# Order of the matrix products inside a weight unit, and one value projection of width 512 in place of two of width 256

## Chip, core, metric

The kernel runs on one core of one Trainium2 chip. The metric is the device time of one execution in microseconds (us), the median of several runs.

## What is computed

A decoder trunk of two layers over 256 positions and 2048 channels, all in float32. Layer 0 (even) has sliding-window attention (A, 16 heads) beside dilated attention (B, 8 heads in three pattern groups that are merged by their softmax denominators); layer 1 (odd) has stick-breaking attention (C) and latent attention (D). Each layer ends with a squared-ReLU MLP of width 8192. Cut to what matters here:

```python
# even layer, w_in is 2048 x 5888; the three dilated groups gi = 0, 1, 2
h = x @ w_in                                       # 256 x 5888
qa, ka, va, hb = split(h, [1024, 1152, 1280])
for gi, (window, dil) in enumerate(((128, 1), (512, 4), (2048, 16))):
    q, k, v = hb[:, gi*1536:(gi+1)*1536] as 3 x 8 heads x 64
    o[gi], lse[gi] = banded_attention(q, k, v, dilation=dil)
ob = sum over gi of softmax(lse)[gi] * o[gi]
x = layer_norm(ALPHA * x + concat(oa, ob) @ w_out)
# every layer
hid = relu(x @ w1);  x = layer_norm(ALPHA * x + (hid * hid) @ w2)
```

## The kernel before

**Weights.** All weights stream through one list, made by `plan` in the order of use. An entry, here called a unit, is 128 x 1024 float32: `block(w, k0, nkt, c0, width)` cuts a column band of the matrix into units of 1024/width row tiles of 128 (a unit of width 512 has two row tiles, of width 256 four). SyncE loads a unit into `raw`; ScalarE casts it to `w_hi` (L120) and VectorE stores the remainder in `w_lo` (L121). Four pairs of `w_hi`, `w_lo` are kept (`spl`), and units are split three ahead of their use.

**Products.** An operand is held as a high and a low part, and a product is hi*hi + hi*lo + lo*hi, summed in PSUM. Two helpers do nearly all of TensorE's work:
- `ws` has the weights as the stationary operand (128 x 128, loaded by one LDWEIGHTS for each product). An activation tile is 128 x 512: 256 columns of high part, then 256 of low part. For each output tile f and each row tile kk it issues one 512-column product of `w_hi` with both parts (L326) and then one 256-column product of `w_lo` with the high part into the upper half of the same bank (L327). A call has a bank for each f. At the last unit, each bank is handed to `take` as soon as it is complete; `take` uses ScalarE and VectorE to join its halves. `ws` serves the query and key projections and the first matrix of both MLPs.
- `as_` has the activations as the stationary operand and streams the weights: three products for each row tile and each half t of the positions (L372 to L374), of the width of the unit. It serves values, output projections and the second matrix of the MLPs.

**Attention steps.** Between two units of a projection the code calls `pump()`, which runs one step of the attention queue on all engines (`attn_step`): the scores of a pair of heads (L694), one transpose of a finished probability tile through the single PSUM tile `pt` (L260, `flip`) with ScalarE's copy to `pT` (L262), or the product of two probability tiles with the values (L279, L281, `weigh`). Steps have a fixed lag behind one another, and one transpose goes out in a step. The queue thus runs in the shadow of the projections, so long as there are units left; `finish(job)` runs the remaining steps one after the other without units between them. An engine takes its instructions in the order in which the code issues them.

**The dilated heads.** `even_b(half, ...)` runs twice, for four heads each. For each group gi it projects q and k (two `ws` calls of width 256), queues the scores, and projects v (`as_`, width 256, four units, each followed by a pump). After the second half come the output projections: columns c = 0, 1 over ten of twelve tiles, then c = 2 over all twelve. The last two tiles are those of the second half; `finish(jb[1])` runs when c = 2 first asks for one, which is ahead of the products of its fifth unit (through `near`, L372's loop).

Of the kernel before, what the change touches and what calls it, by code (L numbers as in the profile page):

```python
# [11 lines left out]
F32 = mybir.dt.float32  # L12
# [6 lines left out]
P = 128  # L19
S = 256  # L20
D = 2048
KT = D // P
# [12 lines left out]
def alibi(n):  # L35
    return [float(v) for v in np.float32(2.0) ** (np.float32(-8.0) * np.arange(1, n + 1, dtype=np.float32) / np.float32(n))]
# [127 lines left out]
class Trunk:  # L164
# [140 lines left out]
    def ws(self, xs, nkt, width, take, more=False):  # L305


        nc = self.nc
        nf = width // P
        if more:  # L310
            banks = [self.ps.tile([P, 512], F32, name=n, bufs=m) for n, m in (("sc", 2), ("sc", 2), ("pt", 1), ("o", 1))]
        else:
            banks = [self.acc() for _ in range(nf)]
        kt = 0
        while kt < nkt:
            self.near(xs, kt, 1024 // width, nkt)
            end = kt + 1024 // width >= nkt
            hi, lo, n, wd = self.w.next(ahead=self.split_ahead - end)
            assert wd == width
            self.near(xs, kt + 2, 1024 // width, nkt)  # L320
            for f in range(nf):
                for kk in range(n):
                    xh, xl, both = xs[kt + kk]
                    c = kk * width + f * P
                    first, last = kt + kk == 0, kt + kk == nkt - 1
                    nc.tensor.matmul(banks[f], hi[:, c:c + P], both, start=first, stop=False, skip_group_check=True)  # L326
                    nc.tensor.matmul(banks[f][:, S:2 * S], lo[:, c:c + P], xh, start=False, stop=last, skip_group_check=True)  # L327
                if kt + n == nkt:
                    take(f, banks[f])
            kt += n  # L330
            if kt < nkt:
                self.pump()
# [47 lines left out]
    def plan(self):  # L380
        a, w = self.a, self.w
        wi = a["even_w_in"][0]
        w.block(wi, 0, KT, 0, 512)
        w.block(wi, 0, KT, 512, 512)
        w.block(wi, 0, KT, 1024, 256)
        for half in range(2):
            for gi in range(3):
                for j in range(3):
                    w.block(wi, 0, KT, 1280 + gi * 1536 + j * 512 + half * 256, 256)
        wo = a["even_w_out"][0]  # L390
        for c in range(3):
            w.block(wo, 0, 10 if c < 2 else 12, c * 512, 512)
        for c in range(2):
            w.block(wo, 10, 2, c * 512, 512)
        w.block(wo, 0, 12, 3 * 512, 512)
        self.plan_mlp(0)
        wi = a["odd_w_in"][0]
        w.block(wi, 0, KT, 3072, 512)
        w.block(wi, 0, KT, 3584, 288)
        w.block(wi, 0, KT, 2048, 512)  # L400
        w.block(wi, 0, KT, 0, 512)
        self.plan_uq(0, 0)
        w.block(wi, 0, KT, 1024, 512)
        self.plan_uq(0, 1)
        w.block(wi, 0, KT, 2048 + 512, 512)
        self.plan_ukv(0)
        w.block(wi, 0, KT, 512, 512)
        self.plan_uq(1, 0)
        w.block(wi, 0, KT, 1024 + 512, 512)
        self.plan_uq(1, 1)  # L410
        self.plan_ukv(1)
        wo = a["odd_w_out"][0]
        for k0s in ((0, 8), (4,), (12,)):
            for c in range(4):
                for k0 in k0s:
                    w.block(wo, k0, 4, c * 512, 512)
        self.plan_mlp(1)
# [324 lines left out]
    def even(self):  # L742
        nc = self.nc
        slopes = alibi(16)
        qa = self.project(512, scale=0.125) + self.project(512, scale=0.125)
        kd = self.tile2()
        va = self.tile2()
        kvf = self.at.tile([P, 2, S], F32, name="kvf", bufs=1)
        vf = kvf[:, 1, :]

        def take(f, bank):
            self.join(kvf[:, f, :], bank)
            if f == 0:
                for kv in range(2):
                    for half in range(2):
                        eng = nc.scalar.copy if half else nc.vector.tensor_copy
                        eng(kd[half * HD:half * HD + HD, kv, :], kvf[kv * HD:kv * HD + HD, 0, :])

        self.ws(self.xT, KT, 256, take)
        self.pump()  # L760

        def flip_v():
            pt = self.ps.tile([P, 384], F32, name="pt")
            for t in range(2):
                nc.tensor.transpose(pt[:, t * P:(t + 1) * P], vf[:, t * P:(t + 1) * P], self.ident)
            nc.vector.tensor_copy(va[:, :, 0:P], pt[:, 0:S].rearrange("p (t c) -> p t c", t=2))

        self.at_step(self.i, 0, flip_v)
        top, power, divide = self.softmax(1, sink=lambda h: self.sinks[:, h:h + 1])

        def score(h, u):
            r = slice((h % 2) * HD, (h % 2) * HD + HD)
            return qa[h // 4][r, (h // 2) % 2, :], kd[r, h // 8, :]

        def bias(h, u, sc, st):
            nc.vector.scalar_tensor_tensor(st, self.masks[:, 0, :], -slopes[h], sc, op0=ALU.mult, op1=ALU.add)
            top(h, st)

        def value(h, u, blk):
            return va[:, blk, (h // 8) * HD:(h // 8) * HD + HD]  # L780

        ja = Job("A", 16, 1, score, (bias, power, divide), value, 5, self.y_at)
        self.queue(ja)
        jb = [self.even_b(0, self.y_at), self.even_b(1, self.x_slot)]
        self.finish(jb[0])
        self.finish_side()
        ys = ja.out + jb[0].out
        st = self.new_stats()

        def rest():  # L790
            self.finish(jb[1])
            yield jb[1].out

        late = LazyTiles(rest())
        late.tiles += ys
        for c in range(3):
            o = self.as_(late if c == 2 else ys, 12 if c == 2 else 10, 512)
            self.add_res(o, c, True, st if c == 2 else None)
            self.pump()
        for c in range(2):  # L800
            o = self.as_(jb[1].out, 2, 512)
            self.add_res(o, c, False, st)
        o = self.as_(late, 12, 512, hold=2)
        return (o, 3, True), st

    def even_b(self, half, y):
        nc = self.nc
        sl = alibi(8)
        qkv = []
        top, power, divide = self.softmax(3)  # L810

        def score(h, u):
            r = slice((h % 2) * HD, (h % 2) * HD + HD)
            return qkv[u][0][r, h // 2, :], qkv[u][1][r, h // 2, :]

        def bias(h, u, sc, st):
            nc.vector.scalar_tensor_tensor(st[:, u * 384:(u + 1) * 384], self.masks[:, 1 + u, :], -sl[half * 4 + h], sc,
                                           op0=ALU.mult, op1=ALU.add)
            if u == 2:
                top(h, st)  # L820

        def value(h, u, blk):
            return qkv[u][2][:, blk, h * HD:h * HD + HD]

        job = Job(f"B{half}", 4, 3, score, (bias, power, divide), value, 4, y)
        for gi in range(3):
            q = self.project(256, scale=0.125)[0]
            k = self.project(256)[0]
            qkv.append((q, k, None))
            self.queue(job, gi)  # L830
            o = self.as_(self.xT, KT, 256)
            v = self.tile2()
            for t in range(2):
                nc.scalar.copy(v[:, t, :], o[t])
            self.pump()
            qkv[gi] = (q, k, v)
        return job

    def project(self, width, tag="qk", scale=1.0):
# [334 lines left out]
```

## Time and profile before

| | |
|---|---|
| median of 3 runs | 2205.27 us (2204.86 to 2205.53) |
| the profiled execution: its time | 2207.19 us |
| its span (first to last instruction) | 2205.4 us |
| outside the span | 1.79 us |
| TensorE busy | 2181.4 us (99%), 11611 products |
| weight loads busy (beside the products) | 1833.6 us (83%) |
| VectorE, ScalarE busy | 1400.8 us (64%), 1058.4 us (48%) |
| bytes moved | 399.07 MB, 181 GB/s mean |

A product's duration in the profile holds its way through the array, and products overlap: what a product costs TensorE is the distance from its start to the start of the next, which the timeline shows. The granted TensorE clock was 0.998 of the full 2.4 GHz over the span.

### The profile page before, as it was taken

What the parts mean: (1) busy time and instruction counts of PE and PEld (TensorE: products, weight loads), DVE (VectorE), ACT (ScalarE), POOL (GpSimd) and SP (SyncE); (2) the same over time, 40 slices, a digit from 0 to 9 for tenths busy, and PEclk for the clock granted to TensorE, in tenths of its full rate; (3) what the DMA queues carried; (4) which work ended last, traced back from release to release, by engine and by line L of the source; (5) the groups of instructions that cost most, each with busy time, mean ns of one, the idle gap of its engine ahead of it and who ended that gap; (6) DMA issues with size and microseconds to landing.
All of it is one profiled execution on the core that took longest, in us unless ns stands there. A gap on an engine that the chain in (4) does not pass through costs nothing.

```text
span 2205.4 us, 30048 instructions
## 1 busy us (share of the span) xinstructions
PE 2181.4 (99%) x11611; PEld 1833.6 (83%) x11612; DVE 1400.8 (64%) x1904; ACT 1058.4 (48%) x1524; POOL 53.7 (2%) x80
## 2 busy tenths in 40 slices
PE   9999999999999999999999999999999999999998
PEld 7888887888888888888888787778888888888886
DVE  5766465775465556565567887878645655554656
ACT  4555453444354345344344565635534534443542
POOL 0000000000000000000012101000000000000000
PEclk9999999999999999999999999999999999999999
DMA  7445554565555555555557443455555555556553
GB/s 266 152 137 158 155 171 155 194 198 191 191 183 197 192 185 190 194 179 198 192 154 227 151 130 135 144 197 190 213 195 182 188 196 189 191 192 191 179 198 121
DMA packets 224320, 399.07 MB, mean 181 GB/s; under 512 B 12778, under 2 KB 56512, under 8 KB 223408
## 3 DMA queue, kind: packets, MB, share of 16 engines
q1 hardware_dynamic: 221472, 386.78, 52.9%
q0 software_dynamic: 2416, 9.84, 1.6%
q8 instruction: 91, 1.49, 0.3%
q10 hardware_dynamic: 288, 0.52, 0.1%
q14 instruction: 53, 0.43, 0.1%
HBM read 395.00 MB, written 2.10 MB: 180 GB/s over the span
## 4 chain that ended last, share of the span: by engine, by line
PE 92%; DVE 4%; issue 1%; DMA 1%; ACT 1%; POOL 0%; SPq 0%; POOLq 0%; ACTq 0%; DVEq 0%
PE acc L326 19%; PE acc L372 14%; PE acc L373 14%; PE acc L374 14%; PE acc L327 9%; PE sc L326 5%; PE sc L327 3%; PE pt L326 3%; PE o L326 3%; DVE w_lo L121 1%; PE pt L327 1%; PE o L327 1%; PE sc L694 1%; PE pt L260 1%; PE o L279 1%
## 5 line engine op out<-in xcount | busy, mean ns | idle before, releaser
L121 DVE TENSOR_TENSOR w_lo<-raw,w_hi 128x1024 fp32r<-128x1024 f32 (+2 forms) x748 | 890.9, 1204 | 606.5 <-ACT w_hi L120 602.3
L120 ACT CAST w_hi<-raw 128x1024 fp32r<-128x1024 f32 (+2 forms) x748 | 760.3, 1030 | 759.7 <-PE acc L374 451.5
L326 PE MATMUL acc<-x,w_hi 128*128 128x512 f32 x1824 | 655.5, 402 | 3.4 <-DVE x L515 3.1
L327 PE MATMUL acc<-x,w_lo 128*128 128x256 f32 x1824 | 513.0, 281 | 0.0
L326 PEld LDWEIGHTS acc<-x,w_hi 128*128 128x128 f32 x1824 | 343.9, 189 | 91.4 <-issue 3.6
L372 PE MATMUL acc<-w_hi,h_hi 128*128 128x512 f32 x1016 | 395.4, 389 | 0.0
L373 PE MATMUL acc<-w_lo,h_hi 128*128 128x512 f32 x1016 | 395.3, 389 | 0.0
L374 PE MATMUL acc<-w_hi,h_lo 128*128 128x512 f32 x1016 | 395.3, 389 | 0.0
L327 PEld LDWEIGHTS acc<-x,w_lo 128*128 128x128 f32 x1824 | 345.7, 190 | 0.4
L372 PEld LDWEIGHTS acc<-w_hi,h_hi 128*128 128x128 f32 x1016 | 190.7, 188 | 39.9
L374 PEld LDWEIGHTS acc<-w_hi,h_lo 128*128 128x128 f32 x1016 | 190.7, 188 | 39.7
L373 PEld LDWEIGHTS acc<-w_lo,h_hi 128*128 128x128 f32 x1016 | 190.7, 188 | 39.2
L326 PE MATMUL sc<-x,w_hi 128*128 128x512 f32 x512 | 186.7, 399 | 0.0
L327 PE MATMUL sc<-x,w_lo 128*128 128x256 f32 x512 | 143.8, 281 | 0.0
L372 PE MATMUL acc<-w_hi,x 128*128 128x256 f32 (+2 forms) x400 | 135.6, 339 | 0.3 <-DVE x L514 0.2
L373 PE MATMUL acc<-w_lo,x 128*128 128x256 f32 (+2 forms) x400 | 132.5, 331 | 0.2 <-DVE w_lo L121 0.2
L374 PE MATMUL acc<-w_hi,x 128*128 128x256 f32 (+2 forms) x400 | 132.6, 331 | 0.0
L326 PEld LDWEIGHTS sc<-x,w_hi 128*128 128x128 f32 x512 | 96.2, 188 | 24.1
L338 ACT ACTIVATE xfull<-acc 128x256 f32<-128x256 f32 x130 | 49.7, 384 | 127.1 <-PE acc L327 108.6
L327 PEld LDWEIGHTS sc<-x,w_lo 128*128 128x128 f32 x512 | 96.7, 189 | 0.0
L326 PE MATMUL pt<-x,w_hi 128*128 128x512 f32 x256 | 96.3, 399 | 0.0
L326 PE MATMUL o<-x,w_hi 128*128 128x512 f32 x256 | 96.2, 399 | 0.0
(203 smaller groups left out, 2089.0 us busy)
## 6 DMA issues: line engine op xcount, KB each, us to landing
raw<-in_mlp_w SPq DMA_DIRECT2D x512, 512.0 KB, 3.8
raw<-in_even_w_in SPq DMA_DIRECT2D x92, 512.0 KB, 4.2
raw<-in_odd_w_in SPq DMA_DIRECT2D x56, 512.0 KB, 3.6
raw<-in_odd_w_out SPq DMA_DIRECT2D x32, 512.0 KB, 3.5
raw<-in_even_w_out SPq DMA_DIRECT2D x24, 512.0 KB, 3.8
gb_rows<-in_ln_g POOLq DMA_DIRECT2D x3, 1024.0 KB, 5.0
gb_rows<-in_ln_b POOLq DMA_DIRECT2D x3, 1024.0 KB, 7.1
raw<-in_odd_w_uq SPq DMA_DIRECT2D x8, 384.0 KB, 4.3
```

The costliest lines, as they stand in the source:

```text
L120: nc.scalar.copy(h, r)
L121: nc.vector.tensor_tensor(l, r, h.bitcast(F32), op=ALU.subtract)
L260: nc.tensor.transpose(pt[:, b * P:(b + 1) * P], st[:, u * 384 + b * P:u * 384 + (b + 1) * P], self.ident)
L279: nc.tensor.matmul(o[rows, :], v, w[:, 0:S], start=first, stop=False, skip_group_check=True)
L326: nc.tensor.matmul(banks[f], hi[:, c:c + P], both, start=first, stop=False, skip_group_check=True)
L327: nc.tensor.matmul(banks[f][:, S:2 * S], lo[:, c:c + P], xh, start=False, stop=last, skip_group_check=True)
L338: nc.scalar.activation(t, bank[:, S:2 * S], AF.Copy, scale=scale)
L372: nc.tensor.matmul(outs[t], xh[:, ts], hi[:, c:c + width], start=first, stop=False, skip_group_check=True)
L373: nc.tensor.matmul(outs[t], xh[:, ts], lo[:, c:c + width], start=False, stop=False, skip_group_check=True)
L374: nc.tensor.matmul(outs[t], xl[:, ts], hi[:, c:c + width], start=False, stop=last, skip_group_check=True)
L694: nc.tensor.matmul(sc[:, cols], q[:, qs], k[:, ks], start=True, stop=True, skip_group_check=True)
```

## The change

In `ws`, the products of a unit are put in another order. In a unit that is not a call's last, first all eight 512-column products (f outer, kk inner) and then all eight 256-column ones. In the last unit each f has its 512-column products and then its 256-column ones, ahead of its `take`: runs of two (width 512) or four (width 256). No product is added or taken away.

In the dilated heads, the values of both halves are projected in half 0, with units of width 512 (eight of two row tiles in place of two times four of four). The second half's values are kept in three new tiles `vb`. Half 1 has no value projection and so no pumps from one. `as_` itself is as before; its three products are L375 to L377 in the changed file, and those of `ws` L326 and L329.

```diff
     def ws(self, xs, nkt, width, take, more=False):
...
-            for f in range(nf):
-                for kk in range(n):
-                    xh, xl, both = xs[kt + kk]
-                    c = kk * width + f * P
-                    first, last = kt + kk == 0, kt + kk == nkt - 1
-                    nc.tensor.matmul(banks[f], hi[:, c:c + P], both, start=first, stop=False, skip_group_check=True)
-                    nc.tensor.matmul(banks[f][:, S:2 * S], lo[:, c:c + P], xh, start=False, stop=last, skip_group_check=True)
-                if kt + n == nkt:
-                    take(f, banks[f])
+            ends = kt + n == nkt
+            for fs in ([[f] for f in range(nf)] if ends else [range(nf)]):
+                todo = [(f, kk, kk * width + f * P) for f in fs for kk in range(n)]
+                for f, kk, c in todo:
+                    nc.tensor.matmul(banks[f], hi[:, c:c + P], xs[kt + kk][2], start=kt + kk == 0, stop=False,
+                                     skip_group_check=True)
+                for f, kk, c in todo:
+                    nc.tensor.matmul(banks[f][:, S:2 * S], lo[:, c:c + P], xs[kt + kk][0], start=False,
+                                     stop=kt + kk == nkt - 1, skip_group_check=True)
+                if ends:
+                    take(fs[0], banks[fs[0]])
...
     def plan(self):
...
-                for j in range(3):
+                for j in range(2):
                     w.block(wi, 0, KT, 1280 + gi * 1536 + j * 512 + half * 256, 256)
+                if half == 0:
+                    w.block(wi, 0, KT, 1280 + gi * 1536 + 1024, 512)
...
     def even_b(self, half, y):
...
-            o = self.as_(self.xT, KT, 256)
-            v = self.tile2()
-            for t in range(2):
-                nc.scalar.copy(v[:, t, :], o[t])
-            self.pump()
-            qkv[gi] = (q, k, v)
+            if half == 0:
+                o = self.as_(self.xT, KT, 512)
+                vs = [self.tile2(), self.at.tile([P, 2, S], F32, name="vb", bufs=3)]
+                for j, v in enumerate(vs):
+                    for t in range(2):
+                        nc.scalar.copy(v[:, t, :], o[t][:, j * S:(j + 1) * S])
+                self.vb.append(vs[1])
+                self.pump()
+                qkv[gi] = (q, k, vs[0])
+            else:
+                qkv[gi] = (q, k, self.vb[gi])
```

**A unit on TensorE.** These are rows of TensorE's program in the first query projection, its third unit, before. A row names the line, the operation, the bank `acc` that is written, the activation tile `x2` and the split weights; the two row tiles of the unit share a name.

```order
L502 MATMUL sc_214<-ident_88,x_res_90 128x128 x4
L326 MATMUL acc_117<-x2_181,w_hi_168 128x512
L327 MATMUL acc_117<-x2_181,w_lo_169 128x256
L326 MATMUL acc_117<-x2_181,w_hi_168 128x512
L327 MATMUL acc_117<-x2_181,w_lo_169 128x256
L326 MATMUL acc_118<-x2_181,w_hi_168 128x512
L327 MATMUL acc_118<-x2_181,w_lo_169 128x256
```

The same unit in the changed program, whole (`x2` at the end of a row: two in a row that read alike):

```order
L507 MATMUL sc_214<-ident_88,x_res_90 128x128 x4
L326 MATMUL acc_117<-x2_181,w_hi_168 128x512 x2
L326 MATMUL acc_118<-x2_181,w_hi_168 128x512 x2
L326 MATMUL acc_119<-x2_181,w_hi_168 128x512 x2
L326 MATMUL acc_120<-x2_181,w_hi_168 128x512 x2
L329 MATMUL acc_117<-x2_181,w_lo_169 128x256 x2
L329 MATMUL acc_118<-x2_181,w_lo_169 128x256 x2
L329 MATMUL acc_119<-x2_181,w_lo_169 128x256 x2
L329 MATMUL acc_120<-x2_181,w_lo_169 128x256 x2
```

The widths alternated product by product; now they change twice in a unit of sixteen products.

**The end of the dilated heads.** These are the last attention steps of half 1 on TensorE before, ahead of the fifth unit of column c = 2 of the output projection (`y`: attention outputs; S: probability tile):

```order
L260 MATMUL pt<-ident,S 128x128 x3
L372 MATMUL acc<-w_hi,y 128x512
L373 MATMUL acc<-w_lo,y 128x512
L374 MATMUL acc<-w_hi,y 128x512
...
L279 MATMUL o<-pT,qk 64x256 x2
L281 MATMUL o<-pT,qk 64x128 x2
L372 MATMUL acc<-w_hi,y 128x512
```

And the last steps of half 1 in the changed program, in the same place:

```order
L377 MATMUL acc<-w_hi,y 128x512
L279 MATMUL o<-pT,vb 64x256 x2
L281 MATMUL o<-pT,vb 64x128 x2
L260 MATMUL pt<-ident,S 128x128 x6
L279 MATMUL o<-pT,vb 64x256 x2
L281 MATMUL o<-pT,vb 64x128 x2
L260 MATMUL pt<-ident,S 128x128 x3
L279 MATMUL o<-pT,vb 64x256 x2
L281 MATMUL o<-pT,vb 64x128 x2
L375 MATMUL acc<-w_hi,y 128x512
```

Before, twelve products of a unit or more stood between any two transposes of half 1. Now half 1's last value projection and its four pumps are gone, and `finish` still has four steps to run, so that two of the transposes (the row with `x6` is two tiles of three) and two `weigh` steps have no unit before them.

## Rows read from the trace of the kernel before

**Rows 1.** The page: busy time by engine; the chain by engine, by line.
```profile
PE 2181.4 (99%) x11611; PEld 1833.6 (83%) x11612; DVE 1400.8 (64%) x1904; ACT 1058.4 (48%) x1524; POOL 53.7 (2%) x80
...
PE 92%; DVE 4%; issue 1%; DMA 1%; ACT 1%; POOL 0%; SPq 0%; POOLq 0%; ACTq 0%; DVEq 0%
```

**Rows 2.** Groups by line and form: operation, shapes, count; busy us, mean ns; idle before.
```profile
L326 PE MATMUL acc<-x,w_hi 128*128 128x512 f32 x1824 | 655.5, 402 | 3.4 <-DVE x L515 3.1
...
L372 PE MATMUL acc<-w_hi,x 128*128 128x256 f32 x192 | 55.9, 291 | 0.0
...
L326 PEld LDWEIGHTS acc<-x,w_hi 128*128 128x128 f32 x1824 | 343.9, 189 | 91.4 <-issue 3.6 <-ACT w_hi L120 2.9 <-DVE x L515 2.7
```

**Rows 3.** Timeline, TensorE, MLP's first matrix: start us, duration, line, operation.
```profile
440.07 0.40 PE L326 MATMUL sc<-x,w_hi 128*128 128x512 f32 x1
440.31 0.28 PE L327 MATMUL sc<-x,w_lo 128*128 128x256 f32 x1
440.42 0.40 PE L326 MATMUL sc<-x,w_hi 128*128 128x512 f32 x1
...
464.45 0.40 PE L326 MATMUL acc<-x,w_hi 128*128 128x512 f32 x1
```

**Rows 4.** Timeline, TensorE, MLP's second matrix: products of 512 columns alone.
```profile
739.65 0.39 PE L373 MATMUL acc<-w_lo,h_hi 128*128 128x512 f32 x1
...
760.27 0.39 PE L374 MATMUL acc<-w_hi,h_lo 128*128 128x512 f32 x1
```

**Rows 5.** Timeline, TensorE, a value projection: products of 256 columns alone.
```profile
273.91 0.28 PE L373 MATMUL acc<-w_lo,x 128*128 128x256 f32 x1
...
279.43 0.28 PE L374 MATMUL acc<-w_hi,x 128*128 128x256 f32 x1
```

**Rows 6.** Timeline, TensorE, layer 1's `ukv`: twelve 256-column products, then six of 512.
```profile
1277.20 0.28 PE L997 MATMUL acc<-y,w_hi 128*128 128x256 f32 x1
...
1278.14 0.28 PE L996 MATMUL acc<-y,w_hi 128*128 128x256 f32 x1
...
1278.50 0.40 PE L1002 MATMUL acc<-w_hi,y 128*128 128x512 f32 x1
...
1279.66 0.39 PE L1004 MATMUL acc<-w_hi,y 128*128 128x512 f32 x1
```

**Rows 7.** Timeline, TensorE: first 512-column runs after alternation, at two places.
```profile
495.89 0.40 PE L372 MATMUL acc<-w_hi,h_hi 128*128 128x512 f32 x1
...
498.45 0.39 PE L374 MATMUL acc<-w_hi,h_lo 128*128 128x512 f32 x1
...
673.43 0.40 PE L372 MATMUL acc<-w_hi,h_hi 128*128 128x512 f32 x1
...
674.59 0.39 PE L374 MATMUL acc<-w_hi,h_lo 128*128 128x512 f32 x1
```

**Rows 8.** Timeline, TensorE: from a run of 512 columns to a 256-column product.
```profile
582.99 0.39 PE L326 MATMUL acc<-x,w_hi 128*128 128x512 f32 x1
583.22 0.28 PE L327 MATMUL acc<-x,w_lo 128*128 128x256 f32 x1
583.33 0.40 PE L326 MATMUL acc<-x,w_hi 128*128 128x512 f32 x1
```

**Rows 9.** Timeline, TensorE and ScalarE, a late attention step in the output projection.
```profile
361.33 0.55 PE L260 MATMUL pt<-ident,S 128*128 128x128 f32 x3
361.64 0.48 PE L372 MATMUL acc<-w_hi,y 128*128 128x512 f32 x1
361.95 0.40 PE L373 MATMUL acc<-w_lo,y 128*128 128x512 f32 x1
...
364.27 0.39 PE L374 MATMUL acc<-w_hi,y 128*128 128x512 f32 x1
...
361.97 0.48 ACT L262 COPY pT<-pt 128x384 f32<-128x384 f32 x1 [2.63 <-PE pt L260]
362.35 1.05 ACT L120 CAST w_hi<-raw 128x1024 fp32r<-128x1024 f32 x1
```

More of the change, by code (lines that the diff above doesn't have):

```diff
@@ L780, in value @@
             return va[:, blk, (h // 8) * HD:(h // 8) * HD + HD]
+        self.vb = []
         ja = Job("A", 16, 1, score, (bias, power, divide), value, 5, self.y_at)
```

## Prediction

> **What bounds the kernel.** I read the page first. TensorE is busy 99% of the span and carries 92% of the chain that ended last [rows 1]; VectorE, ScalarE and the transfers have a third of their time or more to spare. So the time is the number of products times what each costs TensorE, and only that. The groups by line then say which products there are, but their mean durations (402 ns for 512 columns, 291 for 256 [rows 2]) can't be added: products overlap. The timeline gives the cost, from start to start. In `ws`, where the widths alternate, 69 pairs lie between the first and the last row of [rows 3]: 24.38 us, or 353.3 ns a pair. Where only 512-column products follow each other, 91 steps take 20.62 us, 226.6 ns each [rows 4]. Where only 256-column ones do, 46 steps take 5.52 us, 120.0 ns each [rows 5]. One of each, unmixed, would be 346.6 ns: **alternation costs 6.7 ns a pair**. The operands differ between these rows (in [rows 3] weights are stationary, in [rows 4, 5] activations), but the twelve 256-column products of `ukv` at the start of [rows 6] are stationary weights, and end at the same 0.12 us.
>
> **Part 1, the order in `ws`.** By the code, `ws` is called 38 times with width 512 (8 units) and 13 times with width 256 (4 units); each unit has 8 pairs, 2848 in all, of which the 1824 of [rows 2] write `acc` and the rest the banks `sc`, `pt` and `o`. All have the order changed: 38 x 7 + 13 x 3 = 305 units get runs of eight, 51 last units get runs of two or four.
>
> A run of eight costs 8 x 346.6 = 2773 ns against 8 x 353.3 = 2826 now, so 53 ns could come back, if a change of width were free. The rows say it isn't quite. After 256-column products, 512-column ones start slowly: the five steps from 1278.50 to 1279.66 [rows 6] take 1.16 us, 27 ns more than 5 x 226.6, before they settle. The same 27 ns stand after alternation in the second pair of [rows 7] (1.16 us for five), while the first pair there has 2.56 us for eleven steps, 67 ns too much. The other change costs nothing: from the last 512-column product of a run to the 256-column one is 0.23 us, and the next step only 0.11 [rows 8], 10 ns under 120; the first eight steps of [rows 6] are 0.94 us, 20 ns under. So a unit pays between 0 and 67 ns, less 0 to 20. I take 27, seen right behind a 256-column run, less the 10 of [rows 8]: 2790 ns, **36 ns saved a unit**.
>
> Counted on the changed program, 63 of the 305 units come right after an attention step or a layer norm's transposes. There 512-column products stay slow for longer: ten steps from 361.95 to 364.27 take 2.32 us, 5.4 ns too much each [rows 9], so 43 ns for eight in place of 27; I take 20 ns saved. For a last unit of width 512 there are four changes of width with runs of two; by the first two steps of a slow start (0.24 and 0.23, some 14 ns) less 10 it saves up to 36 ns, by nothing but the pairs that stop alternating (4 of 8) 27, by the slower start of [rows 7] nothing. I take 13. Sum: 242 x 36 + 63 x 20 + 51 x 13 = 8.7 + 1.3 + 0.7 = **10.7 us less**. The bounds: with free changes 305 x 53 + 51 x 27 = 17.5 us less; with 67 ns and no credit each unit loses 14 ns, 4.3 us more.
>
> The first thing a reader should ask is whether a product covers the load of the next weights. A LDWEIGHTS record lasts 189 ns [rows 2], longer than the 120 ns step of the 256-column products, and yet these keep their 120 ns; so the record isn't what a load holds up. The Trainium skill, "TensorE: Matmul & The Clock Gate", section "LDWEIGHTS (loading the stationary operand)", gives a load the number of its columns over 1.2 GHz, an estimate of 107 ns for 128. By that rule every product here covers the next load in either order, the order has no say, and part 1 would be nothing; by the rows it is 10.7 us. The rows don't contradict the 107 ns, but the 6.7 ns of alternation and the slow starts have no place in it.
>
> Nothing else on the path moves with the order. `w_lo` is wanted later in a unit than before and `w_hi` is given back earlier; both were ready in time (TensorE stood idle 3.4 us in all ahead of 1824 of the first products of a pair, for an activation tile [rows 2]). Each `take` keeps its place behind its own bank.
>
> **Part 2, the values.** For each group, 192 products of 256 columns become 96 of 512: 96 x (2 x 120.0 - 226.6) = 1.29 us, 3.9 us for three. Seven of the 24 new units follow transposes and pay 12 x 5.4 = 65 ns each, 0.5 us, so **3.4 us less**. The units of the weight stream are as many and as large; the twelve copies out of PSUM are the same number, on ScalarE, off the path.
>
> **The steps that lose their cover.** Half 1 loses four pumps behind its last scores, so four steps that ran between units are left to `finish`. Their work on TensorE is not new; what is new is that TensorE waits for ScalarE, as there is one `pt` tile. Covered, a transpose starts at 361.33, its copy at 361.97 for 0.48 us, and behind it ScalarE has a cast of 1.05 us [rows 9]. Uncovered, the transpose after it can't start before about 1.2 us where 0.31 would do: 0.85 us idle. The cast issued for the fifth unit stands ahead of the second copy, which ends some 2.65 us after the first transpose; `weigh` fills until 2.3: 0.4 us idle. The last `weigh` waits for the third copy: 0.85 us. Together **2.1 us more**; at least 0.8 (one wait), at most 4 if a cast gets ahead of each copy. Behind it the `y` copy and subtraction have the fifth unit's twelve products (2.7 us) as cover.
>
> **Sum.** -10.7 - 3.4 + 2.1 = -12.0 us. The profiled execution took 2207.19 us (span 2205.4 and 1.79 around it) and would take 2195.2. The median of the three runs is 1.92 us under the profiled one; I carry the difference over: **2193.3 us**.
>
> **Rivals.**
> 1. *Order makes no difference.* The 6.7 ns belong to the products of `ws` (two widths into one bank) or every unit gives back 53 ns at its changes of width, near the 67 of [rows 7]. For it: no row shows eight stationary-weight products of 512 columns in a run. Against it: [rows 6] with 27. Left are -3.4 + 2.1: 2204.0 us. The Trainium skill's rule on loads, above, comes out at the same time.
> 2. *Changes of width are free.* A unit's 256-column run gains what the 512-column run loses, as the 0.94 us in [rows 6] suggest (20 of 27). Then -17.5, -3.9 and only 0.8 for the tail: 2184.7 us.
> 3. *Slower.* Each return from 256 to 512 columns pays the long start, 67 ns in eleven steps. The point from which it decides is 53 ns a unit. At 67 the 305 units lose 4.3 us; the 38 last units of width 512, with four returns each (two first steps of 0.24 us, 25 ns, nothing given back), lose some 46 ns each, 1.7 us; with part 2 and the tail +4.7 us: 2210.0 us. For it: the first pair of [rows 7]. Against: of the eight switches from `ws` to the MLP's second matrix in the timeline only two look like it, the other six like the second pair.
>
> **Chances.** The forecast (a unit saves 20 to 45 ns) 0.62, with its own range 2188 to 2199; rival 1 0.17; rival 2 0.15; rival 3 0.06. 0.2% of the time is 4.4 us, about what a measurement of this kernel can tell from no change, so faster means under 2200.9: the forecast, rival 2 and a little of rival 1's spread, 0.79; same 0.16; slower 0.05. The range reaches to rival 1 and to rival 2: 2185 to 2204.
>
> **What would show it.** In the timeline of a `ws` unit: eight starts 226 to 236 ns apart, settling, then one step of about 0.11 us and seven of 0.117 to 0.120, a unit of 2.79 us where it was 2.83. The MLP's first matrix (2048 of the pairs) should shorten by some 8 us of part 1. In the value projections: 512-column steps of 0.227 in half 0, none in half 1. Ahead of the fifth unit of column c = 2: three waits of TensorE between transposes of under a microsecond each, with the clock still granted in full. The prediction is wrong if a run of eight 512-column products keeps steps of 0.235 to its end, if 256-column runs fall over 0.12, or if the tail waits several microseconds.

## The result and the profile after

The changed kernel takes 2194.11 us (median of 6 runs, 2193.77 to 2194.51) against 2205.58 us (6 runs beside it, 2204.86 to 2206.26): a ratio of 0.9948, 95% interval 0.9935 to 0.9961. It is 11.5 us faster; 12.0 were forecast, and 2193.3 us.

The page after, busy time by engine and the chain by engine [rows 1]:

```profile
PE 2165.6 (99%) x11324; PEld 1818.2 (83%) x11324; DVE 1398.8 (64%) x1904; ACT 1057.8 (48%) x1524; POOL 53.5 (2%) x80
...
PE 92%; DVE 4%; issue 1%; DMA 1%; ACT 1%; POOL 0%; SPq 0%; POOLq 0%; ACTq 0%; DVEq 0%
```

TensorE bounds the kernel as before, and has 287 products fewer on record (288 by the program: 576 of 256 columns became 288 of 512).

A unit of the MLP's first matrix, in the timeline of TensorE (start, duration of the merged row, line, count). Before, such a unit was a row for each product [rows 3]:

```profile
581.14 2.00 PE L326 MATMUL acc<-x,w_hi 128*128 128x512 f32 x8
582.98 1.12 PE L329 MATMUL acc<-x,w_lo 128*128 128x256 f32 x8
583.93 2.00 PE L326 MATMUL acc<-x,w_hi 128*128 128x512 f32 x8
...
588.57 1.11 PE L329 MATMUL acc<-x,w_lo 128*128 128x256 f32 x8
```

Read the starts, not the durations: eight 512-column products take 1.84 us, where eight unmixed ones [rows 4] would take 1.813, and eight 256-column ones 0.95, where unmixed ones [rows 5] would take 0.96. The unit is 2.79 us; it was 2.83. The slow start of 27 ns and the credit of 10 ns were read from other places before [rows 6 to 8], and here they stand.

A call's last unit, in runs of two, takes 2.79 us as well, from its first row to the first of the next unit:

```profile
597.90 0.63 PE L326 MATMUL acc<-x,w_hi 128*128 128x512 f32 x2
598.37 0.39 PE L329 MATMUL acc<-x,w_lo 128*128 128x256 f32 x2
...
600.69 1.09 PE L326 MATMUL sc<-x,w_hi 128*128 128x512 f32 x4
```

The best ruler in these traces is one MLP quarter: 512 products, from the first product of `ws` to the first of the second matrix. Before it was 582.99 to 673.43 [rows 7, 8], 90.44 us. After:

```profile
578.37 1.98 PE L326 MATMUL acc<-x,w_hi 128*128 128x512 f32 x8
...
667.71 0.40 PE L375 MATMUL acc<-w_hi,h_hi 128*128 128x512 f32 x1
```

89.34 us, 1.10 less. The timeline holds six quarters of this kind, each with the same gain, and two that begin with a layer norm's transposes and gain some 1.35 us each: 9.3 us of the whole.

The end of the dilated heads on TensorE, where before a unit followed each transpose [rows 9]:

```profile
359.64 0.65 PE L279 MATMUL o<-pT,vb 128*64 128x256 f32 x4
...
360.44 0.55 PE L260 MATMUL pt<-ident,S 128*128 128x128 f32 x3
361.61 0.55 PE L260 MATMUL pt<-ident,S 128*128 128x128 f32 x3 [0.62 <-ACT pT L262]
362.09 0.65 PE L279 MATMUL o<-pT,vb 128*64 128x256 f32 x4
...
362.94 0.55 PE L260 MATMUL pt<-ident,S 128*128 128x128 f32 x3
363.41 1.12 PE L279 MATMUL o<-pT,vb 128*64 128x256 f32 x3
...
364.90 0.50 PE L375 MATMUL acc<-w_hi,y 128*128 128x512 f32 x1
```

The same stretch on ScalarE:

```profile
361.08 0.48 ACT L262 COPY pT<-pt 128x384 f32<-128x384 f32 x1 [2.63 <-PE pt L260]
361.46 1.05 ACT L120 CAST w_hi<-raw 128x1024 fp32r<-128x1024 f32 x1
362.40 0.48 ACT L262 COPY pT<-pt 128x384 f32<-128x384 f32 x1
363.58 0.48 ACT L262 COPY pT<-pt 128x384 f32<-128x384 f32 x1 [0.69 <-PE pt L260]
```

The second transpose starts 1.17 us after the first, and its row names the copy it waited for. The third comes right behind `weigh`, without a wait. The last `weigh` takes from 363.41 to 364.90, 1.49 us, where a covered one takes 0.80 (359.64 to 360.44): its second head's copy starts only at 363.58. From 360.44 to 364.90 are 4.46 us; three transposes of 0.31 [rows 9] and two `weigh` of 0.80 are 2.53. So the uncovered steps cost up to 1.9 us; some 0.3 of it is given back, since four returns from a step to a unit are gone, each with a first product of 0.31 us in place of 0.23 [rows 9].

### The profile page after: what moved, and what is told of

The parts are those of the page before. It is cut to its first block, busy times and chain, and to the rows that moved or that the text cites. A ratio compares the mean times of both kernels' runs of the same rounds, so it can differ in the third digit from the quotient of the medians.

```text
span 2191.9 us, 29478 instructions
## 1 busy us (share of the span) xinstructions
PE 2165.6 (99%) x11324; PEld 1818.2 (83%) x11324; DVE 1398.8 (64%) x1904; ACT 1057.8 (48%) x1524; POOL 53.5 (2%) x80
## 4 chain that ended last, share of the span: by engine, by line
PE 92%; DVE 4%; issue 1%; DMA 1%; ACT 1%; POOL 0%; SPq 0%; POOLq 0%; ACTq 0%; DVEq 0%
PE acc L326 19%; PE acc L375 14%; PE acc L377 14%; PE acc L376 14%; PE acc L329 10%; PE sc L326 5%; PE sc L329 3%; PE pt L326 3%; PE o L326 3%; PE o L329 1%; PE pt L329 1%; DVE w_lo L121 1%; PE sc L699 1%; PE pt L260 1%; PE o L279 1%
## 5 line engine op out<-in xcount | busy, mean ns | idle before, releaser
L326 PE MATMUL acc<-x,w_hi 128*128 128x512 f32 x1824 | 477.5, 397 | 4.4 <-DVE x L520 4.4
L375 PE MATMUL acc<-w_hi,h_hi 128*128 128x512 f32 x1016 | 395.4, 389 | 0.0
L377 PE MATMUL acc<-w_hi,h_lo 128*128 128x512 f32 x1016 | 395.3, 389 | 0.0
L326 PEld LDWEIGHTS acc<-x,w_hi 128*128 128x128 f32 x1824 | 323.1, 189 | 63.2 <-ACT w_hi L120 4.4
L329 PEld LDWEIGHTS acc<-x,w_lo 128*128 128x128 f32 x1824 | 259.5, 190 | 25.3
L329 PE MATMUL acc<-x,w_lo 128*128 128x256 f32 x1824 | 266.2, 282 | 0.0
L377 PEld LDWEIGHTS acc<-w_hi,h_lo 128*128 128x128 f32 x1016 | 190.7, 188 | 39.6
L375 PEld LDWEIGHTS acc<-w_hi,h_hi 128*128 128x128 f32 x1016 | 190.7, 188 | 39.3
L326 PE MATMUL sc<-x,w_hi 128*128 128x512 f32 x512 | 142.5, 395 | 0.0
L375 PE MATMUL acc<-w_hi,x 128*128 128x512 f32 (+1 forms) x304 | 119.7, 394 | 0.3 <-DVE x L519 0.2
L376 PE MATMUL acc<-w_lo,x 128*128 128x512 f32 (+1 forms) x304 | 116.4, 383 | 0.2 <-DVE w_lo L121 0.2
L377 PE MATMUL acc<-w_hi,x 128*128 128x512 f32 (+1 forms) x304 | 116.3, 383 | 0.0
L326 PEld LDWEIGHTS sc<-x,w_hi 128*128 128x128 f32 x512 | 86.8, 190 | 10.0
L329 PEld LDWEIGHTS sc<-x,w_lo 128*128 128x128 f32 x512 | 80.5, 189 | 11.6
L329 PE MATMUL sc<-x,w_lo 128*128 128x256 f32 x512 | 83.8, 281 | 0.0
L326 PE MATMUL pt<-x,w_hi 128*128 128x512 f32 x256 | 79.5, 392 | 0.0
L326 PE MATMUL o<-x,w_hi 128*128 128x512 f32 x256 | 79.0, 390 | 0.0
```

Of the source, the lines that this page charges most:

```text
L326: nc.tensor.matmul(banks[f], hi[:, c:c + P], xs[kt + kk][2], start=kt + kk == 0, stop=False, skip_group_check=True)
L329: nc.tensor.matmul(banks[f][:, S:2 * S], lo[:, c:c + P], xs[kt + kk][0], start=False, stop=kt + kk == nkt - 1, skip_group_check=True)
L375: nc.tensor.matmul(outs[t], xh[:, ts], hi[:, c:c + width], start=first, stop=False, skip_group_check=True)
L376: nc.tensor.matmul(outs[t], xh[:, ts], lo[:, c:c + width], start=False, stop=False, skip_group_check=True)
L377: nc.tensor.matmul(outs[t], xl[:, ts], hi[:, c:c + width], start=False, stop=last, skip_group_check=True)
```

## The experiments

Theory: a product costs its columns and a fixed amount, and what alternation costs on top is the change of width, paid as a slow start of the 512-column products behind 256-column ones. Rivals: the order has no say (the gain lies in the values); or what counts is not the width but the alternation of `w_hi` and `w_lo`, or of whole and half banks.

**Only the order** (the diff of `ws` alone, on the kernel before).

> Only the order in ws is changed; the values are projected as before. Theory: a change of width is what costs; runs of eight pay one slow start (about 28 ns) less about 8 ns, runs of two about 15 less 8, where alternation pays 6.7 ns a pair. So 305 units save about 34 ns and the last units about 27: 11.5 us less, 2194 us, and the MLP's first-matrix stretches of 512 products take 89.3 us where they took 90.4. Rival 1, the order has no say and the gain comes from the values and from attention steps that moved: 2205 us, stretches of 90.4.

```profile
581.36 0.62 PE L325 MATMUL acc<-x,w_hi 128*128 128x512 f32 x2
...
670.69 0.40 PE L374 MATMUL acc<-w_hi,h_hi 128*128 128x512 f32 x1
```

2195.53 us against 2205.8 (ratio 0.9953, 0.994 to 0.9967): 10.3 us less, where 11.5 were expected. A quarter takes 89.33 us by the timeline. The order carries about nine tenths of the gain. Rival 1 of the prediction has fallen.

**Only the values** (the other two pieces of the diff, with `ws` as before).

> Only the value projection is changed (512 wide, both halves in half 0); ws alternates as before. Theory: about 3 us less in the value projections, about 1.6 us more in the last attention steps that lose their cover: 2204.2 us, the same within the measurement; the trace shows a wait of TensorE of some 0.8 us between two transposes ahead of the fifth unit of column c = 2. Rival: the lost cover costs as much as or more than the values give, 2206 us or more. Other rival: this part carries most of the gain, 2196 us.

```profile
582.07 0.39 PE L327 MATMUL acc<-x,w_hi 128*128 128x512 f32 x1
...
672.51 0.40 PE L373 MATMUL acc<-w_hi,h_hi 128*128 128x512 f32 x1
```

The quarter is 90.44 us, as before. 2204.52 us against 2205.8, ratio 0.9994 (0.9985 to 1.0002): within the uncertainty of the measurement. The trace has the same tail; from the start of the first value projection to the first transpose of the layer norm ahead of the MLP it takes 297.33 us where the kernel before takes 298.58. First the kernel before, then this run:

```profile
99.51 0.37 PE L372 MATMUL acc<-w_hi,x 128*128 128x256 f32 x1
...
398.09 0.33 PE L502 MATMUL sc<-ident,x_res 128*128 128x128 f32 x1 [0.55 <-DVE x_res L599]
```

```profile
99.82 0.49 PE L373 MATMUL acc<-w_hi,x 128*128 128x512 f32 x1
...
397.15 0.33 PE L505 MATMUL sc<-ident,x_res 128*128 128x128 f32 x1 [0.54 <-DVE x_res L602]
```

That is 1.25 us less, the net of the values' gain, the tail's cost and small shifts elsewhere.

This trace holds something else. In layer 1, whose code is the same in both kernels, the MLP's first quarter alternates without the cost: 196 pairs in 67.95 us, 346.7 ns each, as cheap as unmixed.

```profile
1505.15 0.39 PE L327 MATMUL acc<-x,w_hi 128*128 128x512 f32 x1
...
1573.10 0.39 PE L373 MATMUL acc<-w_hi,h_hi 128*128 128x512 f32 x1
```

In the trace of the kernel before these 196 pairs take 69.25 us, 353.3 ns each; but there, too, one stretch runs free, 62 pairs in 21.49 us, 346.6 ns each:

```profile
34.75 0.40 PE L326 MATMUL acc<-x,w_hi 128*128 128x512 f32 x1
...
56.24 0.40 PE L326 MATMUL acc<-x,w_hi 128*128 128x512 f32 x1
```

So alternation costs 6.7 ns a pair in most stretches of these traces, but it need not. What decides between the two is not shown.

**Runs of two in all units** (on the kernel before).

```diff
-            for f in range(nf):
-                for kk in range(n):
+            ends = kt + n == nkt
+            for fs, ks in [((f,), range(k, k + 2)) for f in range(nf) for k in range(0, n, 2)]:
+                todo = [(f, kk, kk * width + f * P) for f in fs for kk in ks]
...
```

> In the kernel before, all units of ws get runs of two: two 512-column products, two 256-column ones, and so on. Theory of slow starts: a run of two pays 14.7 less 8.0 ns, so a unit of four such runs pays 27 ns where alternation pays 53 and runs of eight 20: the 512-product stretches of the MLP take 89.6 us, the whole 2197 us. Rival: what counts is that all low products of a unit come behind all high ones (each bank's low products far from its high ones): then nothing of the gain is left, stretches of 90.4 us.

Timeline of TensorE, the start of a quarter and its end:

```profile
581.02 0.61 PE L325 MATMUL acc<-x,w_hi 128*128 128x512 f32 x2
581.47 0.40 PE L328 MATMUL acc<-x,w_lo 128*128 128x256 f32 x2
581.70 0.63 PE L325 MATMUL acc<-x,w_hi 128*128 128x512 f32 x2
...
670.18 0.40 PE L374 MATMUL acc<-w_hi,h_hi 128*128 128x512 f32 x1
```

89.16 us, better than the 89.6 expected and than the 89.34 of runs of eight; 2194.56 us in the whole (ratio 0.995, 0.9936 to 0.9963), without the new value projection. The rival has fallen: high and low products of a bank stand close together here, and the gain is whole. But the additive picture of slow starts is wrong for runs of two. The last units of the changed kernel could have told: they are runs of two, and take 2.79 us.

**Serpentine** (on the changed kernel: every second unit of a call starts with its 256-column products).

```diff
+                for low in ((1, 0) if not ends and (kt // n) % 2 else (0, 1)):
+                    for f, kk, c in todo:
+                        if low:
...
```

> The changed kernel, but every second unit of a ws call (its last one apart) starts with its 256-column products, so that runs of sixteen arise across units and the slow starts in a call of eight units fall by three. Theory: each slow start that is left out saves 20 ns: 38 x 3 + 13 x 1 = 127 of them, 2.5 us less than the changed kernel, 2191.6 us; stretches of 512 products in the MLP 89.1 us where the changed kernel has 89.3. Rival, the rest that is lost in a unit doesn't hang on the number of width changes (it is the unit's own): 2194.1 us, stretches of 89.3.

```profile
578.40 0.62 PE L331 MATMUL acc<-x,w_hi 128*128 128x512 f32 x2
...
667.50 0.40 PE L377 MATMUL acc<-w_hi,h_hi 128*128 128x512 f32 x1
```

89.10 us, where 89.1 was expected: twelve returns from 256 to 512 columns fewer in a quarter save 0.24 us, 20 ns each. 2192.82 us (ratio 0.9941, 0.9929 to 0.9954), where 2191.6 were expected: 1.3 us under the changed kernel's 2194.11 (of another set of runs), about half of the 2.5.

**Runs of four in all units** (on the kernel before: `for g in range(0, nf, 4 // n)`, eight pairs in two runs).

> The kernel before, with runs of four in all units of ws: four 512-column products, four 256-column ones, twice in a unit. If a run pays the start of its kind as the first products of a run of eight show it (22 less 8 ns for a run of four), a unit pays 30 ns and the 512-product stretches of the MLP take 89.7 us. If, as runs of two showed (13 ns a unit, stretches of 89.16), the slow start grows with the number of 256-column products that stand before it, a unit pays less than the 20 ns of runs of eight: stretches at or under 89.3.

```profile
580.95 0.62 PE L326 MATMUL acc<-x,w_hi 128*128 128x512 f32 x2
...
600.57 1.09 PE L326 MATMUL acc<-x,w_hi 128*128 128x512 f32 x4
601.50 0.64 PE L329 MATMUL acc<-x,w_lo 128*128 128x256 f32 x4
...
670.73 0.40 PE L376 MATMUL acc<-w_hi,h_hi 128*128 128x512 f32 x1
```

89.78 us and, in its one run, 2199.01: worse than runs of two and of eight. The first picture (89.7) holds here, and the second, which I had made from runs of two, does not.

**No wide product** (on the kernel before).

```diff
-                    nc.tensor.matmul(banks[f], hi[:, c:c + P], both, start=first, stop=False, skip_group_check=True)
+                    nc.tensor.matmul(banks[f][:, 0:S], hi[:, c:c + P], xh, start=first, stop=False, skip_group_check=True)
+                    nc.tensor.matmul(banks[f][:, S:2 * S], hi[:, c:c + P], xl, start=False, stop=False, skip_group_check=True)
```

> In ws of the kernel before, each 512-column product is cut into two of 256 columns, so that all three products of a pair have one width and three weight loads. Theory: without a change of width a product costs its columns and a fixed 13.3 ns, 120.0 each: 360.0 ns for three against 353.3 for the alternating two, stretches of the MLP at 256 x 360.0 = 92.2 us, the whole 2205 + 2848 x 6.7 ns = 2224 us. Rival: the 6.7 ns don't come from the change of width but belong to the alternation of high and low weights or of whole bank and half bank, and stay: 366.7 ns, stretches of 93.9, the whole 2243 us.

```profile
589.32 0.28 PE L326 MATMUL acc<-x,w_hi 128*128 128x256 f32 x1
589.43 0.28 PE L327 MATMUL acc<-x,w_hi 128*128 128x256 f32 x1
...
681.47 0.40 PE L373 MATMUL acc<-w_hi,h_hi 128*128 128x512 f32 x1
```

92.15 us for 768 products, 120.0 ns each: high and low weights alternate still, and cost nothing. The alternation of whole and half banks is gone here, against what the expectation says: each product now writes half a bank. 2227.78 us in its one run (2224 expected; the quarters are as forecast, where the other 4 us lie stays open).

**No narrow product** (on the kernel before: the low product streams `both` into the whole bank).

> In ws of the kernel before, the low product streams all 512 columns too (it adds low times low, which the reference's product also has). The order still alternates high and low weights. Theory: without a change of width a pair costs 2 x 226.7 = 453.3 ns: stretches of the MLP at 256 x 453.3 = 116.1 us, the whole 2205 + 2848 x 0.100 = 2490 us. Rival, as above, the alternation of high and low weights costs 6.7 ns by itself: 460 ns, stretches of 117.8, the whole 2509 us.

```profile
661.68 0.39 PE L326 MATMUL acc<-x,w_hi 128*128 128x512 f32 x1
661.90 0.39 PE L327 MATMUL acc<-x,w_lo 128*128 128x512 f32 x1
...
777.73 0.39 PE L372 MATMUL acc<-w_hi,h_hi 128*128 128x512 f32 x1
```

116.05 us for 512 products, 226.7 ns each; 2490.5 us. With one width, stationary weights alternating between high and low run at the pitch that [rows 4] show for stationary activations. So with one width, either one, the cost is gone, and the alternation of high and low weights has fallen as its cause. One rival is left: a 512-column product fills its bank and a 256-column one half of it, so in both runs the change between whole and half banks went together with the change of width. No run parts the two.

**Free banks for the uncovered transposes** (on the changed kernel).

```diff
-        pt = self.ps.tile([P, 384], F32, name="pt")
+        pt = self.acc()[:, 0:384] if self.tail else self.ps.tile([P, 384], F32, name="pt")
...
```

> The changed kernel, but the transposes that are issued while the second half's last steps are run without units between them write banks of acc in place of the one tile pt. Theory: the wait of some 0.8 us between the two transposes in a row was for the copy out of pt; it goes, and what is left is the last weigh's wait for its copy: the stretch from the first of these transposes to the output projection's next product, 4.5 us in the changed kernel, takes some 3.5. Rival: the copies on ScalarE are late by themselves, behind the weight cast, and the wait only moves to weigh: 4.3 us or more. The whole: 2193 against 2194 us, too little to tell from one run; the trace decides.

```profile
361.09 0.55 PE L261 MATMUL pt<-ident,S 128*128 128x128 f32 x3
361.48 0.49 PE L261 MATMUL acc<-ident,S 128*128 128x128 f32 x3
...
363.06 0.55 PE L261 MATMUL acc<-ident,S 128*128 128x128 f32 x3
363.59 1.07 PE L280 MATMUL o<-pT,vb 128*64 128x256 f32 x3
...
365.02 0.50 PE L376 MATMUL acc<-w_hi,y 128*128 128x512 f32 x1
```

The same stretch on ScalarE:

```profile
361.73 0.48 ACT L263 COPY pT<-pt 128x384 f32<-128x384 f32 x1 [2.63 <-PE pt L261]
362.11 1.05 ACT L120 CAST w_hi<-raw 128x1024 fp32r<-128x1024 f32 x1
363.06 0.48 ACT L263 COPY pT<-acc 128x384 f32<-128x384 f32 x1
363.70 0.48 ACT L263 COPY pT<-acc 128x384 f32<-128x384 f32 x1 [0.16 <-PE acc L261]
```

The second transpose now follows the first by 0.39 us; that wait was for `pt`. From first transpose to next unit are 3.93 us, between the 3.5 of the theory and the 4.3 of the rival: part of the wait moved on to the copies, of which the second stands behind the cast. 2193.6 us in one run.

**Together**, beside the changed kernel on the same chip: serpentine, free banks, and runs of two in `uq`, whose 64 pairs still alternated.

> The changed kernel once more, beside the next one on the same chip: 0.9948 of the kernel before, 2194.1 us.

> The serpentine order, the transposes of the uncovered steps in banks of acc, and runs of two in the query up-projection of layer 1 (64 pairs that still alternated) together. Theory, from what each gave in its own trace: 28 x 0.0195 us less in each unit-pair of the MLP as in the serpentine run, about 2 us in the whole; 0.5 us in the uncovered steps; 64 pairs x 5 ns = 0.3 us: 2.5 to 3 us less than the changed kernel, some 2191.5 us, 0.9935 of the kernel before. Rival: what TensorE gains is given back as waits for activations or weights, and the whole stays within 1 us of the changed kernel.

2194.08 us for the changed kernel (2194.01 to 2195.41, ratio 0.9944, 0.9932 to 0.9957) and 2191.95 for the combination (2191.59 to 2192.47, ratio 0.9934, 0.992 to 0.9947): 2.1 us less, of 2.5 to 3 expected, with no overlap of the two sets of runs. The intervals against the kernel before do overlap, since that one scattered from 2204.42 to 2208.03 here.

## Why the prediction was right, step by step

- *TensorE is the bound, so products add up.* Right: a gain of 1.10 us in a quarter is the same in six quarters, and nothing of it was given back.
- *Alternation of widths costs 6.7 ns a pair.* That the cost goes with one width is shown by two runs: 120.0 and 226.7 ns a product, with high and low weights still alternating. Two things limit it: width and use of the bank are not parted, and some stretches alternate at 346.7 ns. The prediction read its 353.3 ns in a stretch of the dearer kind [rows 3], which is the common one.
- *36 ns saved in a unit of runs of eight.* 2.79 us, as forecast; finer, 34 ns by the quarter: 1.10 us less in 28 units of runs of eight and four last ones. Where a 512-column run begins behind 256-column ones, it pays the short start (27 ns) of [rows 6], not the long one (67 ns) of [rows 7]; so rival 3 did not come. Nor did rival 2: the credit is 8 to 10 ns, not 20.
- *Part 1, 10.7 us.* 10.3 measured by itself (the interval allows 7 to 13). Where it lies was forecast less well: the MLP's first matrix gives 9.3 us in the trace, not some 8. The term that was too small is that of the last units: 13 ns were forecast, and 2.787 us in place of 2.826 are 39.
- *Values and tail, 3.4 less 2.1.* 1.3 forecast and 1.3 measured (not clear of the uncertainty), 1.25 in the trace. There the parts can be told apart, by adding the steps from start to start over the stretch. The value products take 71.66 us before and 68.30 with the values alone changed: 3.36 less, as forecast. Transposes and `weigh` take 1.67 more over the stretch (the 1.9 above was an upper bound), so the tail was sized too dear at 2.1. Of its three waits the second (0.4 us) doesn't exist: ScalarE took the second copy at 362.40, earlier than I had it, and `weigh` covered it. The query and key products take 0.59 more, which the prediction put at nothing and whose cause is not shown, and the output projections 0.15 less. That the net is right to 0.1 us is luck: the errors cancel.
- *The sum, 12.0 us.* 11.5 by the medians, but 13.4 between the two profiled executions (2207.19 and 2193.79 us), of which that of the kernel before was 1.6 us over its median. The sum is borne out to some 2 us; that it agrees to 0.5 is luck in part.
- *The first rule a reader might apply*, that every product covers the next load whatever the order, would have given 2204.0 us. The order alone gave 2195.5. The Trainium skill, "TensorE: Matmul & The Clock Gate", section "LDWEIGHTS (loading the stationary operand)", gives a load the time of its columns over 1.2 GHz, an estimate of 107 ns for 128. The 120.0 ns of 256-column products in a row, each with a load of its own, do not contradict it; that section says nothing of what a change of width costs.

Open is why. The price of a return from 256 to 512 columns, from the quarters (less the unmixed 256 x 346.6 ns = 88.73 us, over the number of returns): alternation 1.71 us over 256, 6.7 ns; runs of two 0.43 over 128, 3.4 ns; runs of four 1.05 over 64, 16 ns; runs of eight some 20 ns; runs of sixteen, by the serpentine's difference, 20 ns. From four on it grows and then stays, as a start that settles after five products would have it. That runs of two pay less than single products do fits no picture that I have. Nor is the price of a return fixed: the 196 pairs in the run with the values alone paid nothing for as many returns. No run here tells what in the engine it comes from.

## What to carry to other kernels

Where TensorE is busy without a gap, measure the step from product to product in the timeline for each pattern of widths, and compare it with runs of one width: differences of a few ns, times thousands of products, are microseconds that no wait in the profile shows. Group products of one width, if the order of accumulation allows it; but try run lengths, since runs of two beat runs of four here. Measure the price of a pattern at more than one place, since the same order ran at two speeds here. When work is pulled out of a loop, look at what ran in its shadow: of 3.4 us less in the values, half was eaten by four steps that had lost their cover.

## What was not expected of the hardware

Runs of two were cheaper (89.16 us a quarter) than runs of four (89.78) and, before the serpentine, than runs of eight (89.34). One and the same alternating order ran at 353.3 ns a pair in most stretches and at 346.7 in others, for up to 196 pairs on end. Every product in a run of one width costs its columns at the full clock and the same 13.3 ns: 512 columns 226.7 ns (213.3 at 2.4 GHz), 256 columns 120.0 (106.7), whichever operand is stationary.
